# Output weights split once and kept in DRAM, and an output projection that takes them in pairs

## The chip, the cores and the metric

The kernel runs on one core of a Trainium2 chip. Its time is device microseconds, the median of several runs. A core has five engines that this text names by their short forms: PE multiplies matrices, DVE and ACT work elementwise, POOL and SP here mostly issue transfers. Each engine runs its own list of instructions strictly in order and waits for others by semaphores. Transfers started by POOL travel in one queue, those started by SP in another, and both are served by the same 16 DMA engines.

## The reference

The layer works on x of 2048 tokens by 1024 columns, float32.

```python
h = rmsnorm(x, norm1_w)
proj = h @ w_in                              # 1024 -> 3840
o = concat(hgrn2(proj[:, :2048]), rwkv7(proj[:, 2048:]))   # two recurrences, 512 columns each
x = x + o @ w_out                            # 1024 x 1024
x = x + (silu(gate) * val) @ w_down          # of rmsnorm(x) @ w_up, conv of width 3
out = rmsnorm(x, final_norm_w)
```

The change concerns only `o @ w_out`, the output projection.

## The kernel before

**Precision by splitting.** Each float32 operand of a large product is split into a high part, rounded to the format that PE multiplies fast, and a low part, the rest: ACT copies the high part (`S.copy`, line 243 or 236) and DVE subtracts it from the original (line 244 or 237). `mm3` (lines 259 to 261) then makes three matmuls of 128 by 512: high by high, high by low, low by high. A weight tile of 128 rows by 512 columns thus costs one ACT and one DVE instruction, and needs two tiles of 256 KB in place of one.

**Stages.** The tokens are cut into four blocks of 512 (nb = 0 to 3). In stage 1 three streams are interleaved. `dense` makes the input projection, thirty column groups ("P jobs") per block of 8 `mm3` each; `rw_stream` runs the rwkv7 recurrence in eight steps (`rw_super`), two per block; `hg_stream` runs the hgrn2 one, head by head. After each step of the two recurrences `fill` lets `dense` issue about 2 us of matmuls. A scheduler then orders the instructions of each engine; PE's order contains all three streams, and PE waits at the next instruction whatever else might be ready. When the P jobs of block nb are done and nb is 2 or more, the output projection of block nb-2 comes ahead of them in `dense`: block 0 before the P jobs of block 2, block 1 before those of block 3, block 2 after the last P job. Block 3 is done in stage 2 by other code (`weights`), which the change doesn't touch. Stage 2 is the feed-forward part.

**The output projection of stage 1, `out_block`.** It makes four passes: two halves of the block's 512 tokens (i2) by two halves of the 1024 output columns (dh). A pass has two accumulators in PSUM, one for each 128 tokens (q = 0 and 1), taken from a ring of two banks, `pj`, which the P jobs use too. For each of 8 pieces of the inner dimension (k), it loads a weight tile `woraw` on POOL's queue, splits it into `wh` and `wl`, and makes one `mm3` for q = 0 and one for q = 1. At the end both accumulators are added to rows of x (`xh`) and stored. Each of the three blocks loads the same 16 weight tiles twice, once for each half of its tokens: 96 loads of 256 KB and 96 splits in all.

**Rings.** Raw tiles come from a ring `wraw` of four that `woraw`, `oraw` (the rows of o) and `xh` share; split weights from rings of four `wh` and four `wl`, which the P jobs use too. So up to four raw and four split tiles can be ahead of PE.

**The input weights** are treated in block 0 as the change now treats w_out: each P job loads raw tiles, splits them, multiplies, and stores both parts to DRAM (`Win`, line 556); blocks 1 to 3 load the parts (line 560). At the end of an output block `last()` calls `load(i)`, which takes two places in the rings `wh` and `wl` for the next P job.

**rw_super's tiles.** Each step takes tiles by tags with one buffer each, among them KBT (first `ai`), M (`mk`), UV (`W`), AR and KB. Before its first step these are free.

## Time and profile before

| | |
|---|---|
| median of 3 runs | 2764.86 us (2762.21 to 2767.12) |
| the profiled execution's own time | 2759.43 us |
| its span | 2757.7 us |
| PE busy | 2640.8 us, 96% of the span |
| DVE, ACT, POOL busy | 1897.2, 1350.5, 368.4 us |
| first and last split of w_out in output block 0 | 580.0 and 679.2 us |
| ... block 1 | 929.5 and 1035.3 us |
| ... block 2 | 1287.0 and 1385.0 us |

Times in rows of the trace are from the start of the span. "PE pj L259" is a matmul of line 259 into the tile pj. "Idle before" names the instruction whose end released the waiting one. In a row of a stretch, the columns are the stretch and its length, then for each engine the busy time and number of instructions, then the clock that PE was granted (1.00 is full), the mean busy share of the 16 DMA engines, and GB/s. Matmuls overlap, so busy time overstates what PE does; the distance between the starts of two matmuls is the better measure.

### The profile page before, as it was taken

The page shows a single profiled execution, that of the slowest core. Times are in us where ns is not written, and L with a number is a line of the kernel's source. Part 1 is how long each engine was busy: PE and PEld are TensorE (multiplying, and loading weights), DVE is VectorE, ACT ScalarE, POOL GpSimd, SP SyncE. Part 2 cuts the span into 40 slices and gives each one's busy share as a digit, 9 for nine tenths or more (in the row PEclk, how much of TensorE's full clock was granted, in tenths as well). Part 3 has the DMA queues.
Part 4 walks back from the last instruction along what each step waited for, and adds up shares of the span by engine and source line. Part 5 has one row for each costly group of instructions (what it writes and reads, how often), then busy time and mean ns, then how long its engine had stood idle before and what let it go on. Part 6 is the DMA issues. An engine that isn't in the chain of part 4 may idle for free.

```text
span 2757.7 us, 47918 instructions
## 1 busy us (share of the span) xinstructions
PE 2640.8 (96%) x18059; PEld 2103.5 (76%) x18059; DVE 1897.2 (69%) x3665; ACT 1350.5 (49%) x2164; POOL 368.4 (13%) x660
## 2 busy tenths in 40 slices
PE   7989999998999999999889999998999999999998
PEld 6767777776777767778667788886888888777887
DVE  4856656575465664657557889988997786667656
ACT  5546443444544444334446755455445555445444
POOL 6423222212321123221100000000000000000000
PEclk9999999999999999999999999999999999999999
DMA  8654644355663556944575368746672224999865
GB/s 301 201 151 161 179 127 132 115 144 170 219 181 104 144 161 204 296 127 123 153 272 160 114 200 263 242 148 219 217 232 76 88 86 144 321 331 313 284 196 184
DMA packets 387709, 515.78 MB, mean 187 GB/s; under 512 B 121759, under 2 KB 218389, under 8 KB 387477
## 3 DMA queue, kind: packets, MB, share of 16 engines
q1 hardware_dynamic: 335537, 343.29, 38.8%
q0 software_dynamic: 51872, 169.41, 19.2%
q8 instruction: 142, 2.33, 0.4%
q14 instruction: 90, 0.74, 0.1%
q10 hardware_dynamic: 68, 0.02, 0.0%
HBM read 375.22 MB, written 137.36 MB: 186 GB/s over the span
## 4 chain that ended last, share of the span: by engine, by line
PE 58%; DMA 7%; DVE 5%; issue 4%; ACT 3%; POOL 1%; SPq 1%; ACTq 0%; DVEq 0%; POOLq 0%
PE ua L259 6%; PE ua L261 6%; PE ua L260 5%; PE pj L259 4%; PE pj L261 3%; PE pj L260 3%; PE ud L259 3%; PE ud L260 3%; PE ud L261 3%; PE da L260 2%; PE da L261 2%; PE da L259 2%; DMA woraw<-in_w_out_dram 2%; PE db L259 2%; PE db L260 2%
## 5 line engine op out<-in xcount | busy, mean ns | idle before, releaser
L259 PE MATMUL pj<-hh,wh 128*128 128x512 f32 x960 | 403.9, 421 | 2.1 <-ACT hh L117 1.8
L261 PE MATMUL pj<-hh,wl 128*128 128x512 f32 x960 | 380.5, 397 | 0.0
L260 PE MATMUL pj<-hl,wh 128*128 128x512 f32 x960 | 380.4, 396 | 0.0
L259 PE MATMUL ua<-Bh,uwh 128*128 128x512 f32 x704 | 278.8, 396 | 15.2 <-ACT uwh L243 13.9
L261 PE MATMUL ua<-Bh,uwl 128*128 128x512 f32 x704 | 276.5, 393 | 0.3 <-DVE uwl L244 0.3
L260 PE MATMUL ua<-Bl,uwh 128*128 128x512 f32 x704 | 276.5, 393 | 0.0
L259 PEld LDWEIGHTS pj<-hh,wh 128*128 128x128 f32 x960 | 182.2, 190 | 55.6 <-issue 12.7
L260 PEld LDWEIGHTS pj<-hl,wh 128*128 128x128 f32 x960 | 182.8, 190 | 40.0 <-issue 6.3
L261 PEld LDWEIGHTS pj<-hh,wl 128*128 128x128 f32 x960 | 182.2, 190 | 40.3 <-issue 0.4
L243 ACT CAST uwh<-uraw 128x512 fp32r<-128x512 f32 x220 | 134.4, 617 | 139.7 <-PE ua L260 68.7
L243 ACT CAST dah<-draw 128x512 fp32r<-128x512 f32 x151 | 93.8, 621 | 186.5 <-PE da L260 50.5
L244 DVE TENSOR_TENSOR dal<-draw,dah 128x512 fp32r<-128x512 f32 x151 | 104.0, 689 | 110.9 <-ACT dah L243 109.6
L244 DVE TENSOR_TENSOR uwl<-uraw,uwh 128x512 fp32r<-128x512 f32 x220 | 146.7, 684 | 47.7 <-ACT uwh L243 47.7
L259 PEld LDWEIGHTS ua<-Bh,uwh 128*128 128x128 f32 x704 | 133.4, 189 | 44.7 <-ACT uwh L243 14.5
L261 PEld LDWEIGHTS ua<-Bh,uwl 128*128 128x128 f32 x704 | 133.6, 190 | 30.3 <-DVE uwl L244 2.0
L260 PEld LDWEIGHTS ua<-Bl,uwh 128*128 128x128 f32 x704 | 133.6, 190 | 26.8
L259 PE MATMUL ud<-Bh,uwh 128*128 128x512 f32 x352 | 137.8, 392 | 1.7 <-DVE cv L1369 1.7
L261 PE MATMUL ud<-Bh,uwl 128*128 128x512 f32 x352 | 137.1, 389 | 0.0
L260 PE MATMUL ud<-Bl,uwh 128*128 128x512 f32 x352 | 137.0, 389 | 0.0
L260 PE MATMUL da<-dbl,dah 128*128 128x512 f32 x340 | 133.3, 392 | 1.1 <-DVE dbl L244 1.0
L261 PE MATMUL da<-dbh,dal 128*128 128x512 f32 x340 | 132.4, 389 | 0.0
L259 PE MATMUL da<-dbh,dah 128*128 128x512 f32 x340 | 128.3, 391 | 1.5 <-ACT dbh L243 1.5
(558 smaller groups left out, 6024.0 us busy)
## 6 DMA issues: line engine op xcount, KB each, us to landing
uraw<-in_w_up_dram SPq DMA_DIRECT2D x176, 256.0 KB, 3.3
woraw<-in_w_out_dram POOLq DMA_DIRECT2D x96, 256.0 KB, 3.7
draw<-Sg SPq DMA_DIRECT2D x88, 256.0 KB, 3.5
draw<-Tw SPq DMA_DIRECT2D x88, 256.0 KB, 3.1
gd<-y SPq DMA_DIRECT2D x86, 256.0 KB, 2.9
xt<-x1d SPq DMA_DIRECT2D x32, 512.0 KB, 6.7
draw<-gd SPq DMA_DIRECT2D x63, 256.0 KB, 5.0
draw<-in_w_down_dram SPq DMA_DIRECT2D x63, 256.0 KB, 5.6
```

The lines of the kernel that those rows point to most:

```text
L243: S.copy(hi, src)
L244: V.tensor_sub(lo, src, hi.bitcast(F32))
L259: TE.matmul(acc, lh, rh, start=first, stop=False, skip_group_check=skip)
L260: TE.matmul(acc, lh, rl, start=False, stop=False, skip_group_check=skip)
L261: TE.matmul(acc, ll, rh, start=False, stop=last, skip_group_check=skip)
```

## The change

**Split once.** A generator `split_wout` is driven from the P jobs of block 0, from the second job on, one step for each k. For each half of the columns (dh) it loads the half of w_out into the tile M (two transfers of 1 MB on SP's queue), waits eight steps, splits eight tiles into KBT (high) and KB (low), then UV (high) and AR (low), and stores these four tiles of 1 MB to DRAM as `Wod`, on SP's queue too. These are the tiles that `rw_super` uses, so its first step waits for the stores of the second half. Each `out_block` then loads `woh` and `wol` for each k from `Wod` on POOL's queue, and splits no weights.

**Pairs.** `out_block` takes k in pairs. Both weight pairs are allocated, then q = 0 makes its `mm3` for both k, then q = 1. The addition to x stands right behind the last `mm3` of its own accumulator.

Three places show how the instructions move. The first is SP's list at the start of the program, where `xt` are rows of x and `Ed` is the first transfer of `rw_super`. Before:

```order
L85 DMA xt<-in_x_dram 128x1024 x4
L488 DMA cst<-in_consts_dram 128x1344
L486 DMA w2a_193<-in_rw_w_dram 64x512
L487 DMA w2a_193<-in_rw_a_dram 64x512
L489 DMA g_194<-in_rw_g_dram 128x512
L411 DMA xt<-in_x_dram 128x1024 x4
L727 DMA Ed<-M 32x16x32 x4
```

The same place now:

```order
L417 DMA wod<-in_w_out_dram 128x4x512 x2
L511 DMA w2a_193<-in_rw_w_dram 64x512
L512 DMA w2a_193<-in_rw_a_dram 64x512
L514 DMA g_194<-in_rw_g_dram 128x512
L428 DMA Wod00h<-woh 128x2048
L436 DMA xt<-in_x_dram 128x1024
L428 DMA Wod00l<-wol 128x2048
L428 DMA Wod01h<-woh 128x2048
L428 DMA Wod01l<-wol 128x2048
L417 DMA wod<-in_w_out_dram 128x4x512 x2
L436 DMA xt<-in_x_dram 128x1024 x2
L428 DMA Wod10h<-woh 128x2048
```

Between `cst` and the first `Ed` four loads and eight stores of 1 MB each have come in (three more stores follow the rows shown). Three of the four row tiles of the next block now stand between them, and the fourth stands behind the last store.

The second is POOL's list at the end of output block 0, where `Win280` and `Win281` are the weights of the next P job. Before:

```order
L383 DMA woraw_7267<-in_w_out_dram 128x512
L383 DMA woraw_7289<-in_w_out_dram 128x512
L560 DMA wl_7282<-Win280l_320 128x512
L560 DMA wh_7281<-Win280h_319 128x512
L560 DMA wh_7285<-Win281h_321 128x512
L560 DMA wl_7286<-Win281l_322 128x512
L383 DMA woraw_7307<-in_w_out_dram 128x512
```

The same place now:

```order
L386 DMA woh_7263<-Wod11h_213 128x512
L386 DMA wol_7264<-Wod11l_214 128x512
L585 DMA wl_7288<-Win280l_328 128x512
L585 DMA wh_7287<-Win280h_327 128x512
L585 DMA wh_7291<-Win281h_329 128x512
L585 DMA wl_7292<-Win281l_330 128x512
L386 DMA woh_7295<-Wod11h_213 128x512
L386 DMA wol_7296<-Wod11l_214 128x512
L386 DMA woh_7299<-Wod11h_213 128x512
L386 DMA wol_7300<-Wod11l_214 128x512
```

Where one raw load stood behind the next job's weights, the whole last pair (7295 and 7299) does now, and it goes into the places of the ring that the pair before it (7259 and 7263) leaves.

The third is PE's list at the same place. Before, with 7167 and 7168 the accumulators of q = 0 and q = 1, and 7291 and 7309 the last two weight tiles:

```order
L259 MATMUL pj_7167<-wh_7291,hh_205 128x512
L259 MATMUL pj_7168<-wh_7291,hh_205 128x512
L260 MATMUL pj_7167<-wl_7292,hh_205 128x512
L261 MATMUL pj_7167<-wh_7291,hl_206 128x512
L260 MATMUL pj_7168<-wl_7292,hh_205 128x512
L261 MATMUL pj_7168<-wh_7291,hl_206 128x512
L259 MATMUL pj_7167<-wh_7309,hh_205 128x512
L259 MATMUL pj_7168<-wh_7309,hh_205 128x512
```

The same place now, with 7189 and 7215 the accumulators, 7259 and 7263 the third pair and 7295 the first half of the last:

```order
L259 MATMUL pj_7215<-woh_7259,hh_205 128x512
L260 MATMUL pj_7215<-wol_7260,hh_205 128x512
L261 MATMUL pj_7215<-woh_7259,hl_206 128x512
L259 MATMUL pj_7215<-woh_7263,hh_205 128x512
L260 MATMUL pj_7215<-wol_7264,hh_205 128x512
L261 MATMUL pj_7215<-woh_7263,hl_206 128x512
L259 MATMUL pj_7189<-woh_7295,hh_205 128x512
L259 MATMUL pj_7215<-woh_7295,hh_205 128x512
L260 MATMUL pj_7189<-wol_7296,hh_205 128x512
L261 MATMUL pj_7189<-woh_7295,hl_206 128x512
L260 MATMUL pj_7215<-wol_7296,hh_205 128x512
L261 MATMUL pj_7215<-woh_7295,hl_206 128x512
```

Up to the third pair both k of a pair go to one accumulator and then to the other; in the last pair PE still alternates between the accumulators. Three matmuls (of 7263) stand between the last use of 7259 and the first of 7295, which takes its place in the ring. In PE's list the last eleven `mm3` of the block stand without other work between them.

```diff
@@ out_block
-                    accs = [bank("pj") for _ in range(2)]
-                    for k in range(KD):
...
-                        raw = wp.tile([P, 512], F32, tag="wraw", name="woraw", bufs=4)
-                        wload(raw, w_out[0, k * P:(k + 1) * P, dh * 512:dh * 512 + 512])
-                        wh, wl = split(wp, raw, [P, 512], "w", 4)
-                        if k == KD - 2:
-                            xh = [wp.tile([P, 512], F32, tag="wraw", name="xh", bufs=4) for _ in range(2)]
...
-                        for q in range(2):
-                            mm3(accs[q], lhs, (wh, wl), k == 0, k == KD - 1)
...
-                    for q in range(2):
-                        V.tensor_add(xh[q], accs[q], xh[q])
+                    accs, xh = [], []
+                    for k2 in range(0, KD, 2):
+                        ws = []
+                        for k in (k2, k2 + 1):
...
+                            w = tuple(wp.tile([P, 512], F32R, tag="w" + c, name="wo" + c, bufs=4) for c in "hl")
+                            for t_, d_ in zip(w, Wod[dh][k // 4]):
+                                wload(t_.bitcast(F32), d_[:, k % 4, :])
+                            ws.append(w)
                         for q in range(2):
+                            t0 = (i2 * 2 + q) * P
+                            if k2 == 0:
+                                accs.append(bank("pj"))
+                            if k2 == KD - 4:
+                                xh.append(wp.tile([P, 512], F32, tag="wraw", name="xh", bufs=4))
+                                dma(xh[q], x[0, nb * BLK + t0:nb * BLK + t0 + P, dh * 512:dh * 512 + 512])
+                            for k, w in zip((k2, k2 + 1), ws):
...
+                                mm3(accs[q], lhs, w, k == 0, k == KD - 1)
+                                if i2 == 1 and dh == 1 and q == 1:
+                                    next_block(then, k)
+                                    if k == KD - 3 and last is not None:
+                                        last()
+                                if k == KD - 1:
+                                    V.tensor_add(xh[q], accs[q], xh[q])
+                                    dma(x1d[nb][t0:t0 + P, dh * 512:dh * 512 + 512], xh[q])
+                                yield 680
+
+        def split_wout():
+            for dh in range(2):
+                raw = rp.tile([P, 8, BLK], F32, tag="M", name="wod")
+                for q in range(2):
+                    dma(raw[:, 4 * q:4 * q + 4, :],
+                        w_out[0, q * 512:q * 512 + 512, dh * 512:dh * 512 + 512].rearrange("(k p) c -> p k c", p=P))
+                for _ in range(8):
+                    yield
+                for q in range(2):
+                    hi, lo = (rp.tile([P, 4, BLK], F32R, tag=tag, name="wo" + c)
+                              for tag, c in ((("KBT", "h"), ("KB", "l")), (("UV", "h"), ("AR", "l")))[q])
+                    for k in range(4):
+                        split_to(hi[:, k, :], lo[:, k, :], raw[:, 4 * q + k, :])
+                        yield
+                    for t_, d_ in zip((hi, lo), Wod[dh][q]):
+                        dma(d_, t_.bitcast(F32))
@@ dense, in the P job's loop over k
                     next(ahead, None)
+                    if i > 1:
+                        next(early, None)
                     mm3(acc, (wh[:, k % 4, :], wl[:, k % 4, :]), (hh[:, k, :], hl[:, k, :]), k == 0, k == KD - 1)
```

33 lines of the change are left out of this document (13 added, 20 removed).

## The prediction

> **What bounds the kernel.** I read the page's engine table first, then stretches of the windows view, then who waits for the split weights, then single rows of the timeline.
>
> ```profile
> span 2757.7 us, 47918 instructions
> PE 2640.8 (96%) x18059; PEld 2103.5 (76%) x18059; DVE 1897.2 (69%) x3665; ACT 1350.5 (49%) x2164; POOL 368.4 (13%) x660
> ```
>
> PE is the bound over the whole span, and the change leaves it every matmul. So it can gain only where PE waits around the output projection, and lose where PE is made to wait. Stretches at the start, then the three output blocks:
>
> ```profile
> 5.00:10.00 5.00, 0.00 (x0) 0.00 (x0) 0.69 (x1) 2.59 (x5) 2.94 (x6) 1.00 1.06 385
> ...
> 20.00:25.00 5.00, 4.76 (x14) 3.69 (x15) 2.73 (x4) 1.92 (x4) 2.52 (x4) 1.00 0.82 276
> 25.00:30.00 5.00, 5.00 (x28) 4.04 (x27) 3.51 (x5) 3.15 (x5) 1.25 (x3) 1.00 0.21 27
> 30.00:65.00 35.00, 35.00 (x155) 27.86 (x154) 15.54 (x34) 14.88 (x25) 23.16 (x38) 1.00 0.98 346
> 65.00:75.00 10.00, 10.00 (x41) 7.57 (x41) 9.03 (x11) 9.93 (x13) 2.37 (x4) 1.00 0.33 117
> 75.00:100.00 25.00, 24.46 (x156) 19.03 (x156) 21.07 (x36) 11.24 (x17) 13.58 (x22) 1.00 0.73 233
> 580.00:690.00 110.00, 97.34 (x1001) 70.79 (x1000) 66.75 (x155) 50.93 (x85) 21.88 (x41) 0.95 0.55 165
> 930.00:1037.00 107.00, 94.83 (x1047) 71.44 (x1046) 71.99 (x175) 51.99 (x89) 19.32 (x36) 0.96 0.54 156
> 1287.00:1391.00 104.00, 96.59 (x1052) 74.31 (x1052) 68.76 (x177) 46.49 (x82) 16.56 (x31) 0.95 0.48 134
> ```
>
> Two things are to be seen. From 30 to 65 us, where the change puts its copying, PE is full and so are the DMA engines (0.98). In the output blocks the DMA engines are half idle, and PE has gaps and runs at a clock of 0.95.
>
> **The splits that go.** 96 loads are split in the output blocks:
>
> ```profile
> L383 POOL DMA_DIRECT2D woraw<-in_w_out_dram x96: 537/537/564, 321.9 to 1381.3; - x96
> L243 ACT CAST wh<-woraw x96: 601/619/628, 570.4 to 1385.0; 128x512 fp32r<-128x512 f32 x96
> L244 DVE TENSOR_TENSOR wl<-woraw,wh x96: 675/691/694, 573.0 to 1388.2; 128x512 fp32r<-128x512 f32 x96
> ...
> DMA to landing us min/median/max: 2.8/3.7/7.9
> ```
>
> Now 16 splits are made at the start, so ACT loses 80 x 0.619 = 50 us and DVE 80 x 0.691 = 55 us. Neither is full, so the worth is what PE waited for. PE's waits in the three output blocks, in order of time:
>
> ```profile
> PE pj L259 <- ACT wh L243: 5.3, 6, 3.3
> PE hg L977 <- DVE hk L934: 2.8, 1, 2.8
> ...
> PE pj L260 <- DVE wl L244: 1.2, 4, 0.5
> ...
> PE pj L259 <- ACT wh L243: 4.4, 4, 1.8
> PE rw L809 <- DMA TZ<-T0d: 3.4, 2, 3.2
> ...
> PE pj L260 <- DVE wl L244: 0.4, 2, 0.2
> ...
> PE pj L260 <- DVE wl L244: 1.7, 3, 1.3
> ...
> PE pj L259 <- DVE xh L401: 0.7, 1, 0.7
> PE pj L259 <- ACT wh L243: 0.5, 1, 0.5
> ```
>
> Weights and the accumulators' eviction (xh, which the pairs stagger) make 5.3 + 1.2 + 4.4 + 0.4 + 1.7 + 0.7 + 0.5 = 14.2 us. The 2.8 us for hk belongs to it too:
>
> ```profile
> 600.62 0.69 DVE L237 TENSOR_TENSOR hl<-oraw,hh 128x512 fp32r<-128x512 f32 x1 [2.77 <-ACT hh L236]
> 601.23 0.42 DVE L934 TENSOR_SCALAR hk<-hf 128x512 f32<-128x512 f32 x1
> ```
>
> hk is queued on DVE behind a split of oraw, whose ring of raw tiles woraw no longer fills. After such a gap PE is slow for a while, as the second pair of rows shows against the first:
>
> ```profile
> 567.05 0.39 PE L259 MATMUL pj<-hh,wh 128*128 128x512 f32 x1
> ...
> 574.32 0.39 PE L261 MATMUL pj<-hh,wl 128*128 128x512 f32 x1
> ...
> 605.62 0.63 PE L261 MATMUL pj<-wh,hl 128*128 128x512 f32 x1
> 606.04 0.63 PE L260 MATMUL pj<-wl,hh 128*128 128x512 f32 x1
> ```
>
> The first two starts are 32 matmuls apart: 7.27 / 32 = 0.227 us each; the last two are 0.42 us apart. The clocks cost 0.05 x 110 + 0.04 x 107 + 0.05 x 104 = 15 us. Other waits (TZ, 3.4 us) stay and keep it low, so I take a third, 5 us. Gain so far: 14.2 + 2.8 + 5 = 22 us; with no clock gain 17, with all of it 32.
>
> **The loads that come.** A pair is 12 matmuls, 12 x 0.227 = 2.72 us, and needs four loads, 1.05 MB; POOL issues them in 4 x 0.537 = 2.15 us. Rings hold two pairs. A place is used for 9 of the 12 matmuls (2.04 us), and the next load of both parts lands 2 x 0.54 + 3.7 = 4.8 us later, so two pairs take at least 6.8 us, one 3.4: 0.7 us more than PE needs. Recurrence work between pairs covers that nearly everywhere; without cover stand the last three pairs of blocks 0 and 1, 6 x 0.7 = 4 us. Bounds: nothing, or all 48 pairs, 34 us.
>
> The last pair of these two blocks is worse. The next P job's weights take two places first, so its load can be issued only when the third pair's first tile is done, three matmuls (0.68 us) before it is needed: 0.54 + 3.7 - 0.68 = 3.6 us, twice 7 us. The stagger fails there too, as PE still alternates accumulators. Gain of the output blocks: 22 - 4 - 7 = 11 us. Its bounds are 32, were all these loads hidden and the clock full, and 17 - 34 - 7 = -24.
>
> For this wait the Trainium skill (TensorE: Matmul & The Clock Gate, What's actually happening) has a rule that speaks against the change: an idle window of about 3.4 us halves PE's clock, until about 3.4 us of work. The trace shows the half clock after a shorter gap, 2.8 us. By that rule each last pair would cost 1.7 us more, and the gain would be 8 us.
>
> **The copying at the start.** The first P jobs' transfers run on POOL's queue, as the DMA view of 30 to 65 us shows:
>
> ```profile
> DMA packets 3611, 12.10 MB, mean 346 GB/s; under 512 B 667, under 2 KB 667, under 8 KB 3606
> ...
> q0 software_dynamic: 3052, 10.03, 81.6%
> q1 hardware_dynamic: 554, 2.01, 16.0%
> ```
>
> w_out is 4.19 MB and its parts 8.39 MB: 12.58 MB more, on SP's queue. At 346 GB/s that is 36.4 us of all 16 engines, at the 385 GB/s of 5 to 10 us, when both queues worked, 32.7 us. I take 385, since both work here too. Idle DMA time to 75 us is 0.18 x 5 + 0.79 x 5 + 0.02 x 35 + 0.67 x 10 = 12.3 us, and a row tile of x (0.52 MB, 1.4 us) now goes behind the last store. The rest, 32.7 - 12.3 - 1.4 = 19 us, has no cover: POOL's queue gets less, so the P jobs' weights come late, and rw_super waits for its tiles:
>
> ```profile
> 64.06 1.27 ACT L117 ACTIVATE ai<-rw,vt 128x512 f32<-128x512 f32 x2
> ...
> 69.20 1.06 ACT L117 ACTIVATE W<-mk 128x1024 f32<-128x1024 f32 x1
> ...
> 71.01 1.22 DVE L683 TENSOR_TENSOR AR<-rkv,W 128x1024 f32<-128x1024 f32 x1
> ...
> 73.28 1.21 DVE L696 TENSOR_TENSOR KB<-mk,ai 128x1024 f32<-128x1024 f32 x1
> ```
>
> These four overwrite what the last four stores read, so all of it must be out by 64 to 73 us of the old time. Behind ai on ACT stand the next P jobs' splits and evictions; PE stops when its two banks are full. PE, full before and after, cannot make it up. Least: the DMA time idle from 75 to 100 us, 0.27 x 25 = 6.8 us, serves as well, 12 us. Most: 346 GB/s and nothing usable after 65 us, 36.4 - 5.6 = 31 us. The Trainium skill (DMA: Bandwidth & Descriptors, Specifications) states a fabric ceiling of 435 GB/s and a limit of about 358 to a core's share of memory. The trace exceeds the lower for 5 us. By 435 the copying would cost 28.9 us and the loss be 15, by 358 35.1 and 21.
>
> The 16 splits here (10 us of ACT, 11 of DVE) I cost at nothing: both idle some 20 of the 35 us. If they did not, they would come on top. SP's twelve more issues hold up nothing before
>
> ```profile
> 96.70 2.42 SPq L727 DMA_DIRECT2D Ed<-M  x4
> ```
>
> **Sum.** +19 - 11 = +8 us on the profiled execution's 2759.43 us (its span and 1.7 us around it): 2767.4. That execution lies 5.4 us under the median of 2764.86, so I forecast 2773 us.
>
> **Rivals.**
> Faster: the copying mostly slips between the P jobs' own transfers, as bound 12 says, and the output blocks give 22 without new waits: -10, 2755 us. For it speaks the half idle DMA there, against it the 0.98 here. It decides when the start costs less than the blocks give.
> Load-bound blocks: half of the 48 pairs wait 0.7 us, 17 us in place of 4. Then 22 - 17 - 7 = -2 and 19 + 2 = +21, 2786 us. The stretches' DMA share of 0.5 speaks against it, the two-pair ring for it; it decides if loads land 1 us later than the median.
> Cancelled: a start of 12 against 11 leaves 2766 us; a change of 0.2%, 5.5 us, is about what a measurement can tell from none.
>
> **How the numbers follow.** The forecast has 0.46, its own range 2766 to 2784. Faster has 0.27, load-bound 0.15, cancelled 0.12. Slower by over 0.2% is 0.46 + 0.15 = 0.61. The range from 2753 to 2790 leaves out what lies beyond the centres of the two outer cases: about 0.11 of the faster one and 0.06 of the load-bound one.
>
> **What would show it.** Right: DMA share near 1 from 20 to some 85 us; ai near 83 us in place of 64; PE some 19 us emptier before 100 us; no waits for wl in the output blocks, which shorten by about 4 us each; one wait of 3 to 4 us for woh at the end of blocks 0 and 1. Wrong: ai before 75 us, or PE waiting for woh and wol all through the blocks.

## The result, and the profile after

The changed kernel takes 2796.07 us (median of 4 runs, 2794.08 to 2800.97), the kernel before 2763.82 us beside it (4 runs, 2762.21 to 2767.12). The ratio is 1.0118, 95% interval 1.01 to 1.0135: slower by 32 us where 8 were forecast. Both profiled executions lie at an end of their spread: 2759.43 us before, the fastest, 2800.97 us after, the slowest. Their spans differ by 41.5 us, so some 9 us of what the two traces show is spread, not change. Later on, a change is given in us as its ratio less one, times 2765 us.

The first lines of the page after:

```profile
span 2799.2 us, 47711 instructions
PE 2646.2 (95%) x18059; PEld 2104.4 (75%) x18059; DVE 1851.3 (66%) x3585; ACT 1302.5 (47%) x2084; POOL 418.6 (15%) x756
```

PE has the same 18059 matmuls, DVE and ACT have 80 instructions less each, POOL 96 issues more, as the change says. Where the time went is read by finding the same instruction in both traces (start in us):

| the same instruction | before | after | later by |
|---|---|---|---|
| first `Ed` of rw_super | 96.7 | 121.9 | 25.2 |
| last group of `Ed` ahead of output block 0 | 548.6 | 574.8 | 26.2 |
| first P job's eviction behind block 0 | 692.1 | 721.6 | 29.5 |
| last `Ed` ahead of block 1 | 905.3 | 934.6 | 29.3 |
| first P job's eviction behind block 1 | 1048.6 | 1084.9 | 36.3 |
| last `Ed` ahead of block 2 | 1266.6 | 1303.9 | 37.3 |
| first addition of block 3 in stage 2 | 1422.8 | 1462.5 | 39.7 |
| end | 2757.7 | 2799.2 | 41.5 |

25 us are lost before the first `Ed`, and the three output blocks lose 3, 7 and 2 us in place of winning 11 together. The stretches after, with the columns of before (first the start, then the output blocks, moved by what they are late):

```profile
20.00:25.00 5.00, 3.55 (x11) 2.47 (x11) 4.81 (x10) 4.97 (x8) 5.00 (x10) 1.00 1.04 367
25.00:30.00 5.00, 5.00 (x28) 4.21 (x27) 3.44 (x7) 3.48 (x7) 0.91 (x2) 1.00 1.02 362
30.00:65.00 35.00, 28.49 (x119) 22.88 (x118) 15.72 (x32) 12.11 (x22) 14.78 (x24) 0.90 1.02 372
65.00:75.00 10.00, 6.75 (x24) 5.11 (x23) 6.88 (x14) 6.75 (x12) 4.70 (x8) 0.83 1.02 419
75.00:90.00 15.00, 9.51 (x41) 6.36 (x39) 1.90 (x4) 2.44 (x5) 4.99 (x8) 0.95 0.95 362
90.00:95.00 5.00, 4.41 (x6) 2.18 (x7) 4.22 (x7) 4.97 (x7) 1.32 (x2) 0.50 0.50 173
95.00:100.00 5.00, 5.00 (x20) 3.69 (x19) 5.00 (x7) 4.95 (x7) 1.07 (x2) 0.97 0.06 21
606.00:719.00 113.00, 97.46 (x1001) 72.19 (x1000) 48.60 (x123) 31.19 (x52) 37.05 (x70) 0.94 0.74 228
959.00:1073.00 114.00, 97.39 (x1050) 72.34 (x1049) 53.68 (x145) 34.37 (x57) 37.28 (x70) 0.95 0.72 218
1324.00:1431.00 107.00, 95.56 (x1052) 72.30 (x1051) 50.73 (x147) 28.17 (x50) 35.82 (x67) 0.97 0.71 211
```

From 20 to 90 us the DMA engines are full and PE, which was full before, idles. At 95 to 100 us there is a hole in the transfers (0.06): the one that stood at 70 us before. In the output blocks DVE and ACT are emptier by some 18 us each, and the transfers' share has gone from about 0.5 to 0.72. The clock is where it was.

What ACT waited for at the start (waits of 20 to 100 us; before, the wait for wraw was 5.1 us), and its last steps ahead of `ai`:

```profile
ACT wh L243 <- DMA wraw<-in_w_in_dram: 24.8, 6, 7.5
...
ACT woh L236 <- DMA wod<-in_w_out_dram: 5.2, 2, 3.7
```

```profile
80.97 0.62 ACT L243 CAST wh<-wraw 128x512 fp32r<-128x512 f32 x1 [7.46 <-DMA wraw<-in_w_in_dram]
88.18 0.62 ACT L243 CAST wh<-wraw 128x512 fp32r<-128x512 f32 x1 [6.58 <-DMA wraw<-in_w_in_dram]
88.70 0.68 ACT L117 ACTIVATE rkv<-pj,omu 128x512 f32<-128x512 f32 x1
89.28 1.25 ACT L117 ACTIVATE ai<-rw,vt 128x512 f32<-128x512 f32 x2
```

The P jobs' raw weights (`wraw`) come late: from 20 to 100 us they land after a median of 9.7 us, before after 5.0. `ai` does not wait for the store that reads its tile: that store (`Wod10h`) was issued at 61.8 us and landed 12.1 us later, at 73.9. `ai` stands behind the last P job, which waited for its weights.

PE's waits in the three output blocks after (us in total, times, longest; the three blocks one after the other):

```profile
PE pj L260 <- DMA wol<-Wod11l: 4.3, 4, 1.8
PE pj L259 <- DVE xh L405: 3.1, 1, 3.1
...
PE pj L259 <- DMA woh<-Wod11h: 2.3, 1, 2.3
...
PE pj L259 <- DMA woh<-Wod01h: 0.7, 1, 0.7
...
PE pj L260 <- DMA wol<-Wod01l: 0.2, 1, 0.2
...
PE pj L259 <- DMA woh<-Wod11h: 5.3, 4, 2.9
...
PE pj L260 <- DMA wol<-Wod11l: 2.5, 4, 0.9
PE pj L259 <- DMA woh<-Wod01h: 1.9, 1, 1.9
PE pj L259 <- DVE xh L405: 1.5, 1, 1.5
...
PE pj L260 <- DMA wol<-Wod10l: 0.5, 1, 0.5
...
PE pj L259 <- DMA woh<-Wod01h: 2.7, 1, 2.7
...
PE pj L259 <- DMA woh<-Wod11h: 1.0, 1, 1.0
```

The waits for split weights are gone. In their place PE waits for woh and wol: 7.5 us in block 0 (4.3 + 2.3 + 0.7 + 0.2), 10.2 us in block 1, 5.0 us in block 2 with three smaller rows, 22.7 us in all. Another 4.6 us are waits for the addition that frees an accumulator; its row of x (`xh`) lands after a median of 6.1 us in block 0, where before it took 3.2.

### The profile page after: what moved, and what is told of

It is laid out like the page before. It is cut to its first block, busy times and chain, and to the rows that moved or that the text cites. A ratio compares the mean times of both kernels' runs of the same rounds, so it can differ in the third digit from the quotient of the medians.

```text
span 2799.2 us, 47711 instructions
## 1 busy us (share of the span) xinstructions
PE 2646.2 (95%) x18059; PEld 2104.4 (75%) x18059; DVE 1851.3 (66%) x3585; ACT 1302.5 (47%) x2084; POOL 418.6 (15%) x756
## 3 DMA queue, kind: packets, MB, share of 16 engines
q1 hardware_dynamic: 338801, 355.87, 39.7%
q8 instruction: 142, 2.33, 0.3%
## 4 chain that ended last, share of the span: by engine, by line
PE 69%; DMA 14%; DVE 7%; ACT 4%; issue 4%; SPq 1%; POOL 1%; DVEq 0%; ACTq 0%; POOLq 0%
PE pj L259 7%; PE pj L260 7%; PE pj L261 7%; PE ua L259 5%; PE ua L260 5%; PE ua L261 5%; PE ud L261 3%; PE ud L259 3%; PE ud L260 3%; PE hg L1005 2%; PE da L260 2%; PE da L259 2%; PE da L261 2%; PE db L259 1%; DMA wraw<-in_w_in_dram 1%
## 5 line engine op out<-in xcount | busy, mean ns | idle before, releaser
L259 PE MATMUL ua<-Bh,uwh 128*128 128x512 f32 x704 | 278.1, 395 | 16.5 <-ACT uwh L243 15.3
```

Source lines behind the costliest of these rows:

```text
L259: TE.matmul(acc, lh, rh, start=first, stop=False, skip_group_check=skip)
```

## The experiments

The runs on the output blocks alone (e2 to e6, e9, e12 to e14) leave the copying out. Where a kernel leaves out or changes a part of the computation, its expectation says which.

**e1: the copying alone.** `split_wout` is that of the change, `out_block` that of before, and nothing reads Wod.

```diff
+            early = split_wout()
...
+                    if i > 1:
+                        next(early, None)
```

> Only the early copying of the split output weights is added; the output blocks stay as before and never read the copies. Theory (the loss at the start is transfer bandwidth, and the blocks of the change lose about 14 us by themselves): +25 us against the kernel before, all of it before the first rw_super, whose Ed comes near 122 us in place of 96.7, and nothing more behind it. Rival (the late start shifts the recurrences against the output blocks, so the two halves of the change are not additive): the start is the same, but the end is under +15 or over +35 us.

Measured: ratio 1.0101 (1.0079 to 1.0122), +28 us; first `Ed` at 121.7 us. The start alone makes most of the loss.

**e2: the new output blocks alone.** `Wsrc` holds the stored parts of the input weights, `Win`.

```diff
-                            for t_, d_ in zip(w, Wod[dh][k // 4]):
-                                wload(t_.bitcast(F32), d_[:, k % 4, :])
+                            for t_, d_ in zip(w, Wsrc[0][dh * 8 + k][0]):
+                                wload(t_.bitcast(F32), d_.rearrange("p a b -> p (a b)"))
-                    if i > 1:
-                        next(early, None)
```

> Only the new output blocks, without any copying: they load two parts per weight tile from DRAM in pairs, but of the input weights' stored parts, since the output weights' parts do not exist here, so the projected values are not the reference's; sizes, counts and queues are those of the change. Theory: +7 to +14 us against the kernel before (the three blocks' last additions come +3, +7 and +3 us later, one after the other), with PE waiting about 20 us for woh and wol. Prediction's theory: -11 us. Rival of no additivity: within 3 us of the kernel before.

Measured: 1.0019 (1.0004 to 1.0034), +5 us. With e1's 28 it makes 33 of the change's 32: the two parts add, and the rival of no additivity falls. The blocks cost a little, just under the theory's +7, where the prediction had them win 11.

**e3: two loads, the old order.**

```diff
-                        wh, wl = split(wp, raw, [P, 512], "w", 4)
+                        wh, wl = (wp.tile([P, 512], F32R, tag="w" + c, name="wo" + c, bufs=4) for c in "hl")
+                        for t_, d_ in zip((wh, wl), Wsrc[0][dh * 8 + k][0]):
+                            wload(t_.bitcast(F32), d_.rearrange("p a b -> p (a b)"))
```

> As the run with the new blocks alone (two parts per weight tile loaded, no splits, no copying, the input weights' stored parts in place of the output weights', so the values are not the reference's), but each weight tile goes to both accumulators in turn as in the kernel before, and the additions stand at the end of a pass. Theory (the doubled transfers are what the blocks lose): +5 to +14 us, PE again waits some 20 us for the weights. Rival (the pairs are what loses, by bursts of the same accumulator and by their late loads): -10 us or better, with less than 8 us of waits for the weights.

Measured: 1.0 (0.9985 to 1.0014). In the old order two loads cost just what the splits did. Neither expectation is met in its number. Between e3 and e2 lie 5 us, with intervals that touch, so the pairs cost little here.

**e4: pairs, with loads and splits as before.**

```diff
-                            w = tuple(wp.tile([P, 512], F32R, tag="w" + c, name="wo" + c, bufs=4) for c in "hl")
-                            for t_, d_ in zip(w, Wod[dh][k // 4]):
-                                wload(t_.bitcast(F32), d_[:, k % 4, :])
-                            ws.append(w)
+                            raw = wp.tile([P, 512], F32, tag="wraw", name="woraw", bufs=4)
+                            wload(raw, w_out[0, k * P:(k + 1) * P, dh * 512:dh * 512 + 512])
+                            ws.append(split(wp, raw, [P, 512], "w", 4))
```

> Pairs alone: weights are loaded once and split in the output block as before, but go in pairs to one accumulator and then the other. Theory (the doubled transfers are what the blocks lose): within 5 us of the kernel before, waits for split weights like those of before, 8 to 14 us. Rival (the pairs lose): +7 us or more, since a pair must wait for two splits.

Measured: 1.007 (1.005 to 1.009), +19 us: the rival. The order in pairs is no gain by itself. The rival's reason, that a pair needs two splits at once, is not shown: PE's listed waits for split weights are 15.3 us in the three blocks, before 13.5. The clock in block 0 fell from 0.96 to 0.88 (575 to 692 us), by estimate 0.08 x 117 = 9 of the 19 us; where the rest goes stays open.

**e5: pairs with one load and no split.** What the removed splits are worth, if nothing is loaded in their place; the diff is against e2.

```diff
-                            w = tuple(wp.tile([P, 512], F32R, tag="w" + c, name="wo" + c, bufs=4) for c in "hl")
...
+                            w = wp.tile([P, 512], F32R, tag="wh", name="woh", bufs=4)
+                            wload(w.bitcast(F32), Wsrc[0][dh * 8 + k][0][0].rearrange("p a b -> p (a b)"))
+                            ws.append((w, w))
```

> As the run with the new blocks alone (pairs, no splits, no copying, stored parts of the input weights in place of the output weights'), but each weight tile is loaded once and that one tile serves as high and as low part, so the values are not the reference's: the transfers of the blocks are those of the kernel before, and the splits are gone as well. Theory (the second load of each weight tile eats the gain of the splits): 14 to 22 us faster than the kernel before, waits for woh under 6 us in all three blocks. Rival (the pairs or the clock eat the gain): within 7 us of the kernel before, like the run with two loads (+5).

Measured: 0.9892 (0.9872 to 0.9911), -30 us, more than the theory had. The waits for woh did not fall under 6 us (13.7 us by the rows of the three blocks), so they alone are not the second load's price of 35 us (30 + 5). One load without pairs was not run, so this price is one in pairs.

**e14: the second load made, and read by nobody.** Against e5:

```diff
+                            u = wp.tile([P, 512], F32R, tag="wl", name="wol", bufs=4)
+                            wload(u.bitcast(F32), Wsrc[0][dh * 8 + k][0][1].rearrange("p a b -> p (a b)"))
```

> As the run with one load per weight tile (28 us faster than the kernel before; not the reference's values), but the second load is made as well, into a ring of four that no instruction reads: bytes and issues of the change, and no matmul waits for the second part. Theory (latency: a matmul that needs the second part waits for it): 15 to 28 us faster than the kernel before. Rival (bandwidth or POOL's issues: the second load delays the first, the rows and the recurrences' transfers): +5 to -8 us, like the new blocks alone.

Measured: 1.0009 (0.9994 to 1.0023), +2 us, the rival. A load that no matmul waits for takes back all of the 30 us. So the second load need not be late for a matmul to cost. But e14 is not free of waits of its own: POOL, which issues the loads in order, waits for an earlier `wol` to land before it loads into its place, 14.8, 14.8 and 8.0 us in the three stretches below, and none in e2. The same stretches over the output blocks, e5 first, then e14:

```profile
575.00:692.00 117.00, 106.24 (x1111) 82.39 (x1110) 56.44 (x150) 41.39 (x70) 26.39 (x50) 0.99 0.62 189
925.00:1042.00 117.00, 108.00 (x1117) 83.08 (x1116) 55.30 (x144) 41.11 (x69) 25.95 (x49) 0.99 0.63 191
1285.00:1400.00 115.00, 101.89 (x1036) 78.49 (x1035) 52.79 (x122) 36.98 (x65) 16.36 (x30) 0.96 0.65 191
```

```profile
575.00:692.00 117.00, 100.45 (x1031) 76.98 (x1030) 51.69 (x133) 35.39 (x59) 40.21 (x75) 0.96 0.74 240
925.00:1042.00 117.00, 102.80 (x1067) 78.32 (x1066) 57.23 (x158) 34.27 (x57) 38.84 (x72) 0.92 0.71 220
1285.00:1400.00 115.00, 102.26 (x1133) 79.60 (x1132) 55.89 (x164) 28.68 (x51) 37.57 (x70) 0.93 0.65 201
```

The transfers' share rises by some 0.1 in the first two blocks, and the clock falls by 0.03, 0.07 and 0.03: 0.03 x 117 + 0.07 x 117 + 0.03 x 115 = 15 us, an estimate that counts all the time of these stretches. From the last `Ed` ahead of block 0 to the first addition of block 3, e14's trace takes 38 us more than e5's. PE's waits in the three blocks rise from 23 to 41 us, so clock and waits together make 33 of the 38.

What the second load does to other transfers is seen best on SP's queue, where the weights do not travel. In each block the recurrence stores T0d and T1d and loads TZ from T0d. The rows in block 0, first e5, then e2:

```profile
591.90 3.54 SPq L794 DMA_DIRECT2D T0d<-Ti  x2
...
599.79 1.46 SPq L801 DMA_DIRECT2D TZ<-T0d  x2
```

```profile
588.23 4.90 SPq L795 DMA_DIRECT2D T0d<-Ti  x2
...
598.74 3.22 SPq L802 DMA_DIRECT2D TZ<-T0d  x2
```

From the issue of T0d to that of TZ pass 7.9, 6.7 and 6.9 us in the three blocks of e5 and 7.1, 6.3 and 6.7 us before, but 10.5, 10.4 and 11.0 us in e2 and 10.9, 11.5 and 12.0 us in the changed kernel. Outside the output blocks e2 has 6.4 and 6.7 us. Between e5 and e2, PE's waits for woh and wol rise by 6 us, all its waits in the three blocks by 16 us (from 23 to 39), and the clock falls by 0.03 in each of the three stretches, some 10 us of 349.

**e9: both parts by one transfer.** Against e2:

```diff
+                            w = wp.tile([P, 2, 512], F32R, tag="wb", name="wob", bufs=4)
+                            wload(w.bitcast(F32), Wsrc[0][dh * 8 + k][0].rearrange("p c a b -> p c (a b)"))
+                            ws.append((w[:, 0], w[:, 1]))
```

> As the run with the new blocks alone (same values, not the reference's), but high and low part of a weight tile lie side by side and come by one transfer of 512 KB, so POOL issues half as many in the output blocks, 2 x 0.54 us per pair in place of 4 x 0.54, for the same bytes. Theory of the ring (a place that comes free is filled again only after the issues and the landing, so a second load costs by its latency): 8 to 25 us faster than the new blocks alone, that is -3 to -20 us against the kernel before. Rival (bandwidth: the engines carry the doubled bytes no faster): within 4 us of the new blocks alone, +1 to +9.

Measured: 1.004 (1.0027 to 1.0053), +11 us, a little past the rival's +9. Half the issues for the same bytes are no gain, so it is not POOL's time to issue. From T0d to TZ it still takes 10.7 to 12.1 us. The run is 6 us worse than e2, perhaps because the high part now comes only with the low one.

**e12 and e13: rings of five.** First the rings alone, with one raw tile less; the same numbers stand at every other tile of these rings:

```diff
-                            w = tuple(wp.tile([P, 512], F32R, tag="w" + c, name="wo" + c, bufs=4) for c in "hl")
+                            w = tuple(wp.tile([P, 512], F32R, tag="w" + c, name="wo" + c, bufs=5) for c in "hl")
...
-                                xh.append(wp.tile([P, 512], F32, tag="wraw", name="xh", bufs=4))
+                                xh.append(wp.tile([P, 512], F32, tag="wraw", name="xh", bufs=3))
```

> As the run with the new blocks alone (same values, not the reference's), but the two rings of weight parts hold five tiles in place of four, and to make room the ring of raw tiles three in place of four. Theory of the ring: 2.5 pairs in flight bring 6.8 us of latency to 2.7 us a pair, what PE needs, so 10 to 25 us faster than the new blocks alone, -5 to -20 us against the kernel before, unless rows of o come late through the shorter raw ring. Rival (bandwidth): within 5 us of the new blocks alone, or slower.

Measured: 1.0012 (0.9996 to 1.0029), +3 us, the rival. The two largest groups of PE's waits around block 0, then around block 1:

```profile
PE rw L816 <- DMA TZ<-T0d: 9.1, 2, 8.6
PE pj L259 <- DMA woh<-Win140h: 3.9, 1, 3.9
...
PE rw L816 <- DMA TZ<-T0d: 9.3, 2, 8.8
PE pj L259 <- DMA woh<-Win140h: 3.3, 1, 3.3
```

In these two blocks the waits for weights are gone but for the last pair and 0.4 us. But PE now waits 9 us in each for TZ. The rows of o do not hold TZ up on SP's queue: in block 0 T0d is issued at 585.8 us, as soon as its source Ti is done, and TZ at 597.5, in e2 at 598.7. What changed is PE's list. The instruction that needs TZ stands behind 42 matmuls of the output projection in each of the two blocks, in place of 66 and 56 in e2, so PE gets to it 14 and 7 us earlier. The next run was meant to take this wait away by asking for the rows of x later in the first pass, and the last pair's by e6's edit:

```diff
-                            if k2 == KD - 4:
+                            if k2 == (KD - 2 if i2 == 0 and dh == 0 else KD - 4):
-                                    if k == KD - 3 and last is not None:
+                                    if k == KD - 1 and last is not None:
```

> As the run with rings of five (new blocks alone, the input weights' parts, so not the reference's values; raw ring of three), with two more edits: in the first pass of blocks 0 and 1 the rows of x are asked for two weight tiles later, so that the raw ring serves the rows of o first, and the next P job's loads stand behind the last pair. Theory (the second load costs by latency in rings of four): the 9 us waits for TZ shrink under 5 and the whole is 10 to 20 us faster than the kernel before. Rival (bandwidth: whatever wait goes, another takes its place): within 4 us of the kernel before.

Measured: 0.9996 (0.9977 to 1.0014), the rival. A wait of 7.8 us for TZ stays in block 0 (in block 1 it is 0.3), and the whole is no faster than before. Deeper rings did not take the second load's price away. But they change the order of PE's list as well, so these two runs do not tell latency from bandwidth by themselves.

**e6 and e11: the next P job's loads behind the last pair**, on e2 and on the kernel before:

```diff
-                                    if k == KD - 3 and last is not None:
+                                    if k == KD - 1 and last is not None:
```

> As the run with the new blocks alone, but the next P job's loads are asked for behind the last pair of blocks 0 and 1, not in front of its loads; values not the reference's, as there. Theory (each last pair waits 3.5 to 5.6 us since those loads take its place in the ring): 5 to 9 us faster than the run with the new blocks alone, that is -4 to 0 us against the kernel before, and no wait over 2 us for the last woh. Rival (the same wait goes to the next P job, whose weights now come late): within 3 us of the run with the new blocks alone, with a wait of 3 us or more at the first matmul behind the block.

> The kernel before, with one edit: the next P job's loads are asked for behind the last weight tile of output blocks 0 and 1, in place of two tiles earlier. Theory (those loads take two places of the rings of split weights, so the last two splits there come late too): 3 to 6 us faster than the kernel before. Rival (the raw tile is there early enough, so nothing is gained, and the P job's weights come late): within 2 us of it, or slower by 2 to 4 us.

Measured: e6 0.999 (0.9977 to 1.0003), 8 us faster than e2, as the theory had it, so each last pair costs about 4 us. e11 0.9993 (0.9979 to 1.0007), its rival: not told from none. In e6 block 0 still has a wait of 1.5 us for the last woh and one of 3.1 us at a P job's eviction.

**e8: the early copying without its stores.**

```diff
-                    for t_, d_ in zip((hi, lo), Wod[dh][q]):
-                        dma(d_, t_.bitcast(F32))
```

> The run with the early copying alone, without its eight stores: w_out is loaded (4.19 MB) and split by ACT and DVE, but nothing is kept; the output blocks are as before. Theory (bandwidth): of 32.7 us of transfers 10.9 are left, and the loss goes from 25 to 10.9 - 7.7 = about 3 us; first Ed near 100 us. Rival (the 16 splits, costed at nothing, or the tiles of rw_super hold up the start): +12 us or more, first Ed at 109 us or later.

Measured: 1.003 (1.0013 to 1.0046), +8 us; first `Ed` at 106.2 us, 9.5 us late. That lies between the two expectations, and the trace shows a reason:

```profile
50.70 0.62 ACT L236 CAST woh<-wod 128x512 fp32r<-128x512 f32 x1 [7.70 <-DMA wod<-in_w_out_dram]
51.23 0.68 ACT L117 ACTIVATE rkv<-pj,omu 128x512 f32<-128x512 f32 x1
```

ACT stands 7.7 us at a split whose half of w_out has not landed, with the P job's eviction (`rkv`) behind it. The splits' own time is small; their place in ACT's list isn't. The eight stores make the other 20 us of e1's 28 (28 - 8).

**e7 and e10: the copying in block 1**, tile by tile through the raw ring, first (e7, the diff) with the load 8 steps ahead of its split on POOL's queue, then 13 ahead on ACT's:

```diff
-                    if i > 1:
+                    if i > NCOL + 1:
                         next(early, None)
...
+                    raw = wp.tile([P, BLK], F32, tag="wraw", name="wod", bufs=4)
+                    wload(raw, w_out[0, k * P:(k + 1) * P, dh * 512:dh * 512 + 512])
...
+                    hi, lo = (wp.tile([P, BLK], F32R, tag="wraw", name="wod" + c, bufs=4) for c in "hl")
+                    split_to(hi, lo, raw)
...
+                    for t_, d_ in zip((hi, lo), Wod[dh][k // 4]):
+                        wload(d_[:, k % 4, :], t_.bitcast(F32))
```

> The change with its copying moved: one weight tile at a time through the ring of raw tiles, on the queue of POOL, during the P jobs of block 1, where the DMA engines are about half busy. Theory (the start loses 25 us only because its DMA engines are full): the start as before, first Ed near 97 us, and the whole +5 to +9 us against the kernel before, what the new blocks cost alone. Rival (the copying costs as much wherever it stands, by its splits or its place in queues): +20 us or more.

> The change with its copying in block 1 again, but each load of a weight tile is asked for 13 steps ahead of its split, on ACT's own queue; in the first such run ACT waited 22 us in all for these loads and the P jobs of block 1 came 12 us late. Theory (that loss was ACT standing in order behind a late load, not the transfers): block 1's P jobs lose under 4 us and the whole is +5 to +10 us against the kernel before. Rival (the transfers or the added splits cost it): +15 us or more again.

Measured: e7 1.0064 (1.0047 to 1.0081), +18 us; e10 1.0098 (1.0066 to 1.0129), +27 us. So e7 lies between its expectations, and e10 is its rival. The start is as before (`Ed` at 96.8 us in e7), but block 1 loses 12 and 19 us in the traces. ACT's waits in e10 from 290 to 400 us:

```profile
ACT wodh L236 <- DMA wod<-in_w_out_dram: 19.7, 6, 5.3
```

The same thing as in e8; in e7 these waits make 22.0 us. Moving the load ahead in the program did not move it far enough ahead in time: all sixteen splits came within 120 us (266.0 to 385.2). That a better spread would cost little is not shown.

**e15 and e16: split at the first use**, as the kernel does with the input weights: the first two passes of block 0 split, multiply and store (`kept` is the pair before the one just loaded).

```diff
+                            if nb == 0 and i2 == 0:
+                                raw = wp.tile([P, 512], F32, tag="wraw", name="woraw", bufs=4)
+                                wload(raw, w_out[0, k * P:(k + 1) * P, dh * 512:dh * 512 + 512])
+                                split_to(w[0], w[1], raw)
+                            else:
+                                for t_, d_ in zip(w, Wod[dh][k // 4]):
+                                    wload(t_.bitcast(F32), d_[:, k % 4, :])
...
+                            for k, w in kept:
+                                for t_, d_ in zip(w, Wod[dh][k // 4]):
+                                    wload(d_[:, k % 4, :], t_.bitcast(F32))
```

> No early copying: the two passes over the first half of block 0's tokens load and split the output weights as the kernel before did, in pairs, and store both parts on POOL's queue; all later passes load the parts as the change does; the next P job's loads stand behind the last pair. Rings of four. Theory: start as before; block 0 loses 5 to 10 us by its two passes with pairs and splits, and stores, blocks 1 and 2 cost 0 to 5: +5 to +12 us against the kernel before, so 20 us faster than the change. Rival (the stores on POOL's queue hold up the loads behind them): +20 us or more.

> As the run with the copy at the first use, with rings of five weight parts and a raw ring of three, and rows of x later in the first pass. Theory (latency of the rings): blocks 1 and 2 gain 5 to 8 us each, so -5 to +2 us against the kernel before. Rival (bandwidth, or the short raw ring): not faster than the same kernel with rings of four.

Measured: e15 1.0097 (1.0074 to 1.0119), +27 us; e16 1.0063 (1.0043 to 1.0083), +17 us. e15 is its rival; e16 misses both of its expectations. The first pass of block 0 ends 23 and 19 us late in the traces. What of that comes from pairs with splits (e4) and what from stores on the queue of the loads is not told apart. Rings of five, with the two edits that go with them, lose 10 us less.

**e17 and e18: half of each split on POOL**, with the loads and the order of before:

```diff
-                        wh, wl = split(wp, raw, [P, 512], "w", 4)
+                        wh, wl = (wp.tile([P, 512], F32R, tag="w" + c, name="w" + c, bufs=4) for c in "hl")
+                        S.copy(wh, raw)
+                        nc.gpsimd.tensor_sub(wl, raw, wh.bitcast(F32))
```

> The kernel before, with one edit: in the three output blocks of stage 1 the low part of an output weight is subtracted by POOL in place of DVE. Theory (a good part of the splits' cost is DVE, whose queue they delay): 5 to 15 us faster than the kernel before, without the 2.8 us wait for hk. Rival (POOL issues the weights' loads in order, and a subtraction that waits for ACT's copy holds up the loads behind it): +5 us or more, with waits for wl over 5 us in a block.

> As the run with the subtraction on POOL, and the next P job's loads asked for behind the last weight tile of blocks 0 and 1. Theory: 0 to 4 us faster than that run. Rival: within 1 us of it, as the same edit alone was on the kernel before (-2 us, not told from none).

Measured: e17 1.012 (1.0103 to 1.0137), +33 us, the rival; e18 1.0115 (1.0085 to 1.0144), not told from e17. POOL takes 1.29 us for the subtraction where DVE takes 0.69, and the weights' loads are issued behind it:

```profile
L386 POOL TENSOR_TENSOR wl<-woraw,wh x30: 1254/1286/2887, 581.0 to 692.3; 128x512 fp32r<-128x512 f32 x30
```

No version that computes the same beats the kernel before: all that copy lose 17 us or more, and e11, the only other one near it, is not told from it.

## Why the prediction was wrong

The direction was right, and the slower side had 0.61; the size, +32 us for +8, lies outside the range. Both terms of the sum failed, the start by 6 to 9 us and the output blocks by 16.

**The start, +19.** Measured +25 at the first `Ed` in both traces with the copying, +28 (22 to 34) in e1. The 32.7 us of transfers were about right: from 20 to 90 us after, the engines moved 375 GB/s, at which 12.58 MB take 33.5 us. The step that failed is the idle time set against them: 12.3 us of it to 75 us, of which 0.67 x 10 = 6.7 us lie at 65 to 75 us. That hole stands behind `ai`, so it moved along with `ai`: after, it is the row 95 to 100 with 0.06. Without it the same sum is 32.7 - 5.6 - 1.4 = 25.7 us. "Nothing usable after 65 us" stood in the text as a condition of the upper bound, and was the likely case. (That bound, 31, leaves out the 1.4 us that the sum takes off.) The agreement with 25 is closer than the sum deserves: for e8, without the stores, it gives 10.9 - 5.6 = 5.3 us, and 9.5 were measured at the first `Ed`, so it leaves out what late splits add.

**The gates.** `ai` came at 89.28 us, not 83, and not because its tile was still being stored (that store landed at 73.9): it stood behind P jobs whose raw weights were late. The copying lost time by the P jobs' transfers, as the text said first, not by the tiles.

**The 16 splits, costed at nothing.** By their duration that holds; by their place it doesn't. The cover named, ACT's idle time, covers nothing when ACT idles at the head of its list: 5.2 us after, 7.7 us in e8, 22.0 us in e7, 19.7 us in e10.

**The gain of the splits, 22.** Right in sign and too small: with one load and no split the blocks were 30 us faster (e5), near the bound of 32. The full clock came with it (0.99, 0.99, 0.96).

**The loads that come, 4 + 7.** This is the step that failed most: the second load costs 35 us (e2 against e5), in place of 11. The text counted only how late a weight pair is in its ring when POOL issues it. The last pairs were forecast at 7 us and measured at 8 (e6); little of the 35 is theirs, since with one load PE also waits there, 4.7 and 3.0 us (e5). The term that was mis-sized is the other, 4 us, taken because the DMA engines were half busy in the output blocks. The price is paid by other transfers too: of the 16 us of waits that come between e5 and e2, 6 are for weights, and the recurrence's T0d to TZ takes over 10 us in place of about 7. With half the issues the price is no less (e9), and with a second load that no matmul reads it is the same, if POOL's own waits are left aside (e14). The new wait for xh, 4.6 us, is of that kind and was not forecast. T0d and TZ travel on SP's queue, so the service of POOL's single queue is not all of it; that the bytes on the 16 engines are, as the share in the blocks' busiest part (below) suggests, is argued and not isolated.

**The third of the clock loss, 5.** Not one of it came: 0.94, 0.95 and 0.97 after, 0.95, 0.96 and 0.95 before.

**The last pairs and the clock.** The end of output block 0 after:

```profile
696.95 0.50 PE L259 MATMUL pj<-woh,hh 128*128 128x512 f32 x1
699.22 0.65 PE L260 MATMUL pj<-wol,hh 128*128 128x512 f32 x1 [1.76 <-DMA wol<-Wod11l]
699.67 0.63 PE L261 MATMUL pj<-woh,hl 128*128 128x512 f32 x1
...
705.18 0.73 PE L259 MATMUL pj<-woh,hh 128*128 128x512 f32 x2 [2.33 <-DMA woh<-Wod11h]
707.11 0.79 PE L260 MATMUL pj<-wol,hh 128*128 128x512 f32 x1 [1.20 <-DMA wol<-Wod11l]
...
712.71 0.57 PE L261 MATMUL pj<-hh,wl 128*128 128x512 f32 x1
713.11 0.40 PE L259 MATMUL pj<-hh,wh 128*128 128x512 f32 x1
```

The wait for the last pair, 2.33 + 1.20 = 3.5 us, is as forecast (3.6). The pair before it also waits, 1.76 us. Behind that wait, and again behind the last pair up to 713 us, PE starts matmuls 0.43 us apart in place of 0.23; between the two the granted clock is back at 1.00 (704 to 706 us). The rule cited in the prediction (the Trainium skill, TensorE: Matmul & The Clock Gate, What's actually happening) has an idle window of about 3.4 us ahead of the half clock, and about as much work to end it. Here a wait of 1.76 us was enough, and 6 us of work without a wait (707.1 to 713.1) were needed. By the rule the two last pairs would have cost 10.4 us, without it 7; e6 says 8.

**The rate.** The rule cited for the copying (the Trainium skill, DMA: Bandwidth & Descriptors, Specifications) gave, as estimates, a loss of 15 us by its ceiling of 435 GB/s and of 21 by 358. The row of 65 to 75 us shows 419 GB/s, above the one and near the other, and the loss is 25: it was the cover that failed, not the rate.

**The rivals.** "Load-bound blocks" came nearest, at 2786 us; its condition, loads that land 1 us later than the median of 3.7, was met. Its price was still taken from pairs that wait, and its start from the same wrong cover. What "would show it right" came true for the transfers' share and the emptier PE before 100 us, the vanished waits for wl and the wait for woh at the blocks' end. `ai` near 83 us and blocks shorter by 4 us each did not come true, and "PE waiting for woh and wol all through the blocks", named as a sign of error, did.

## What to carry to other kernels

Idle time of the DMA engines covers an added transfer only if it lies ahead of the work that the transfer delays; a hole that exists because of that work moves with it. A load that replaces computation is to be priced by what it does to every other transfer in its stretch, and not only by whether its own consumer waits (6 us of 35 here). An instruction on an engine with idle time is free only if its input is there when its turn comes, since all that is queued behind it waits too (7.7 us in e8).

## What the runs showed of the hardware

A share of 0.74 over output block 0 is an average. The transfers' queues from 605 to 655 us after, in block 0 (packets, MB, share of the 16 engines):

```profile
DMA packets 14263, 14.06 MB, mean 281 GB/s; under 512 B 10174, under 2 KB 10174, under 8 KB 14259
...
q0 software_dynamic: 2880, 9.44, 56.8%
q1 hardware_dynamic: 11379, 4.57, 36.1%
```

Here the engines are 93% busy at 281 GB/s, where the start had 419 GB/s at full share. SP's queue takes 36.1% for 4.57 MB, 7.9% per MB, against 6.0% per MB on POOL's. The many packets under 512 B are a likely reason: in the prediction's view of 30 to 65 us, with 667 of them in place of 10174, SP's queue took 16.0% of 35 us for 2.01 MB, 2.8 us of all engines per MB, against 3.9 here. So little room was left in just the stretch where the weights' bytes were doubled; before, the same part had shares of 0.60 and 0.52 (580 to 606 and 606 to 632 us). Loads of woh and wol land after a median of 4.7 to 7.5 us there, where woraw took 3.7.

A second surprise is how the clock multiplies short waits: between e5 and e14 it makes, by the estimate above, 15 of the 38 us, and behind the three short waits at the end of block 0 some 22 matmuls took 0.2 us more each, 4.4 us beside 5.3 us of waits.
